# Two groups of attention values as one product in seven parts, in a hybrid decoder layer

## Chip, cores and metric

The kernel runs on one core of one Trainium2 chip. The metric is the device time of one execution in microseconds (us), given as the median of several runs.

## The reference

The reference is one decoder layer over 512 tokens of width 1024: a SwiGLU block, a mixer of two branches, and a second SwiGLU block, each with a normalisation before and after. The part that matters here is the attention branch. The normalised input `u` (512 x 1024) is multiplied by `w_in`, and columns 3072 to 4607 of it are the values of three groups of heads, 512 columns for each group:

```python
u = rms_norm(h, mix_norm_pre[l])
proj = u @ w_in[l]
q, k, v, xr, yr, gl = jnp.split(proj, splits, axis=-1)
...
v = v.reshape(B, S, N_GROUPS, HEADS_PER_GROUP, HEAD_DIM)
```

Queries and keys are made in the same way from other columns. Each group then attends with its own dilation, and the three results are merged. All is float32.

## The kernel before

A float32 product is made of three matmuls: each operand is split into a high part (ScalarE copies it into a rounded format) and a low part (VectorE subtracts, `split`, lines 295 to 297), and high x high, high x low and low x high are accumulated in PSUM. A weight of 1024 columns per partition thus costs one ScalarE copy and one VectorE subtraction of 128x1024 before TensorE can use it.

Many products are made with seven block products where eight would be the plain way (a Strassen-like scheme). For this both operands are cut into halves in two directions, and sums of the quarters, called *forms*, are split. `forms_of` (line 576) makes the seven forms of the input, p1 to p7, in three steps: `early` makes three sums (lines 615 to 617), `middle` splits p6 and p5 with one sum between them (620 to 622), `late` splits p7 and p4 (625 and 626). p1, p2 and p3 are parts of the input as it is. `w_forms` (632) makes the forms of a pair of weight tiles, and `seven` (697) runs the products of a pair of query and key tiles.

The weights come as one stream of 1 MB blocks in the order in which they are needed (`stream_plan`, line 101). `raw_of` (234) issues the next block on SyncE's queue into one of two `raw` buffers; `fetch` (254) splits a block's part into one of four `w8` buffers (2 x 1024 columns each).

The order of the instructions on each engine is laid out ahead of time by a list scheduler: it goes by the place in the program, and a block under `tc.high_priority(offset=...)` moves forward by that many instructions. `AHEAD` is 100 and stands around the preparation of weights; `EVAC` is 200 and stands around copies out of PSUM. On the chip each engine then keeps to its order.

The mixer begins while the first block's normalisation ends: `Boundary.block` normalises 128 tokens, `Boundary.turn` (506) transposes them on TensorE and splits them into the input `um`. Then `values(g)` (1072) makes the values of a group: four blocks of 128 tokens, each with its own PSUM bank, over eight chunks of 128 input rows, three matmuls each (lines 1086 to 1088) with 128 tokens of the input as the stationary operand and 512 columns of weights as the moving one. Group 0 goes block by block, because the last blocks of the input are still being normalised; its values are afterwards moved by 16 small DMAs into another order (1108). Groups 1 and 2 go chunk by chunk over all four blocks, and ScalarE copies the four banks out (1102). The steps of the input's forms stand between the groups in the program (lines 1115, 1117, 1122): `early` after group 0, `middle` after group 1, `late` after group 2 and after the preparation of the first pair. Queries and keys (`qk`, 1131) follow, one pair per group and head, each with the next pair's preparation ahead of it (`pair_of`, 1124).

[...] `facc` is a buffer of 128 x 8 x 512 that holds the transposed input while the forms are made.

Of the kernel before, what the change touches and what calls it, by code (L numbers as in the profile page):

```python
# [10 lines left out]
F32 = mybir.dt.float32  # L11
# [5 lines left out]
P = 128  # L17
# [19 lines left out]

LAST = 384
WARM = 10
VALUES = (0, 1, 2)  # L40
QKB = 6
CB = 6
GATE1 = ((), (0, 1), (2, 3, 4), (5, 6, 7))
# [57 lines left out]
def stream_plan():  # L101

    plan = []

    def down(n, a, half):
        for kk in range(part_blocks(a)):
            plan.append((("down", n, a, half, kk), 1024))

    def ffn(n):
        for ev in ffn_order(n):  # L110
            if ev[0] == "std":
                plan.append((("gate", n, ev[1]), 1024))
                plan.append((("up", n, ev[1]), 1024))
            elif ev[0] == "prep":
                plan.append((("gu", n, ev[1]), 2048))
            elif ev[0] == "down":
                down(n, *ev[1:])
            elif ev[0] == "prepd":
                for q in SEVEN_RAW[ev[2]]:
                    plan.append((("dq", n, ev[1], q), 1024))  # L120
        for half in range(2):
            down(n, len(FF_PARTS) - 1, half)

    def values(g):
        for k in range(4):
            plan.append((("v", g, k), 1024))

    def qk(h):
        for g in range(NG):
            plan.append((("pair", g * 4 + h, 12 + g * 4 + h), 2048))  # L130

    ffn(1)
    del plan[:4]
    for k in range(KC):
        plan.insert(k, (("start", k), 512))
    for g in VALUES:
        values(g)
    for h in range(NH):
        qk(h)
    for c in range(0, KC, 2):  # L140
        plan.append((("pair", 52 + c, 53 + c), 2048))
    for m in range(0, KC, 2):
        plan.append((("attn", m), 1024))
    for what, h in LRU_ORDER:
        if what == "gates":
            plan.append((("lru", h), 1024))
        elif (what, h) in PAIRED:
            plan.append((pair_key(what, h), 2048))
        else:
            for c in GATE1[h] if what == "gate1" else (2 * h, 2 * h + 1):  # L150
                plan.append((("in", COLUMN[what] + c), 1024))
    for m in range(KC):
        plan.append((("rec", m), 1024))
    for half in range(2):
        for kk in range(4):
            plan.append((("out", half, kk), 1024))
    ffn(2)
    return plan
# [25 lines left out]
def hybrid_layer(ctx: ExitStack, tc: tile.TileContext, xT: bass.AP, xN: bass.AP, wst: bass.AP,  # L184
# [46 lines left out]
    groups = stream_groups()  # L231
    state = {"g": 0, "i": 0, "off": 0, "raw": None, "ahead": AHEAD}

    def raw_of(key):

        g, i = state["g"], state["i"]
        grp = groups[g]
        if i == 0:
            w = grp[-1][1] + grp[-1][2]
            raw = wpool.tile([P, RAW_W], F32, name="raw", tag="raw", bufs=2)  # L240
            src = bass.AP(tensor=wst.tensor, offset=wst.offset + state["off"], ap=[[w, P], [1, w]])
            nc.sync.dma_start(raw[:, :w], src)
            state["raw"] = raw
            state["off"] += w * P
        k, o, w = grp[i]
        assert k == key, (k, key)
        src = state["raw"][:, o:o + w]
        if i + 1 == len(grp):
            state["g"], state["i"] = g + 1, 0
        else:  # L250
            state["i"] = i + 1
        return src

    def fetch(key, slot=None, ahead=0):

        with tc.high_priority(offset=ahead if slot else state["ahead"]):
            src = raw_of(key)
            w = src.shape[-1]
            t = slot() if slot else w8() if w > 512 else w4()
            split(t[:, 0, :w], t[:, 1, :w], src)  # L260
            return t[:, 0, :w], t[:, 1, :w]
# [795 lines left out]
    with ExitStack() as mx:  # L1057
# [11 lines left out]

        vals = {}  # L1070

        def values(g, first=False):
            if g:
                vals[g] = apool.tile([P, 4, T], F32, name="vals", tag=f"v{g}")
            else:
                vals[g] = tpl.tile([P, 8, T], F32, name="vals", tag="attn")[:, 0:4, :]
            ws = [fetch(("v", g, k)) for k in range(4)] if first else [None] * 4
            pss = [acc_ps() for _ in range(4)] if g != VALUES[1] else [aux_ps(), aux_ps(), aux_ps(), acc_ps()]

            def part(kk, bs):  # L1080
                wh, wl = (w.rearrange("p (k c) -> p k c", k=2) for w in ws[kk])
                for b in bs:
                    bl = slice(b * P, (b + 1) * P)
                    for i in range(2):
                        k = 2 * kk + i
                        PE.matmul(pss[b], um.hi[k][:, bl], wh[:, i, :], start=k == 0, stop=False)  # L1086
                        PE.matmul(pss[b], um.hi[k][:, bl], wl[:, i, :], start=False, stop=False)  # L1087
                        PE.matmul(pss[b], um.lo[k][:, bl], wh[:, i, :], start=False, stop=k == KC - 1)  # L1088

            if first:  # L1090
                for b in range(4):
                    for kk in range(4):
                        part(kk, (b,))
                    if b < 2:
                        bd1.turn(b + 2)
                    ACT.activation(vals[g][:, b, :], pss[b], AF.Copy)
            else:
                for kk in range(4):
                    ws[kk] = fetch(("v", g, kk))
                    part(kk, range(4))  # L1100
                for b in range(4):
                    ACT.activation(vals[g][:, b, :], pss[b], AF.Copy)
            if g == 0:

                nv = apool.tile([P, 4, T], F32, name="vals", tag="vn")
                for b in range(4):
                    for p in range(4):
                        nc.gpsimd.dma_start(nv[32 * p:32 * p + 32, b, :], vals[g][32 * b:32 * b + 32, p, :])
                vals[g] = nv

        t, steps = forms_of(um, um_t[:2], um_t[2:], apool, False, rec_half)
        values(VALUES[0], True)
        attn_t = tpl.tile([P, 8, T], F32R, name="attn", tag="attn")
        attn = Act([attn_t[:, i, :] for i in range(4)], [attn_t[:, 4 + i, :] for i in range(4)])
        steps[0]()
        values(VALUES[1])
        steps[1]()
        values(VALUES[2])
        pairs = [[(g * 4 + hd, 12 + g * 4 + hd) for g in range(NG)] for hd in range(NH)]
        order = [("pair",) + p for ps in pairs for p in ps] + [("pair", 52 + c, 53 + c) for c in range(0, KC, 2)]  # L1120
        forms = {order[0]: w_forms(order[0])}
        steps[2]()

        def pair_of(key):

# [433 lines left out]
def _block(key, a):  # L1559
    kind = key[0]  # L1560
    if kind in ("gate", "up"):
        return _cols(a[f"ffn{key[1]}_w_{kind}"], key[2] * P)
    if kind in ("down", "out"):
        if kind == "out":
            w, r0, half = a["w_out"], key[2] * 2 * P, key[1]
        else:
            w, r0, half = a[f"ffn{key[1]}_w_down"], (FF_PARTS[key[2]][0] + key[4] * 2) * P, key[3]
        return w[r0:r0 + 2 * P, half * T:(half + 1) * T].reshape(2, P, T).transpose(1, 0, 2)
    if kind == "dq":
        half, i = "gu".index(key[3][0]), int(key[3][1])  # L1570
        r0 = (FF_PARTS[key[2]][0] + 2 * i) * P
        return a[f"ffn{key[1]}_w_down"][r0:r0 + 2 * P, half * T:(half + 1) * T].reshape(2, P, T).transpose(1, 0, 2)
    if kind == "gu":
        u, g = (_cols(a[f"ffn{key[1]}_w_{k}"], key[2] * P) for k in ("up", "gate"))
        return np.concatenate([u, g], axis=1)
    if kind == "in":
        return _cols(a["w_in"], key[1] * P)
    if kind == "v":
        return _cols(a["w_in"][key[2] * 256:(key[2] + 1) * 256], 3072 + key[1] * 512, 512)
    if kind == "pair":  # L1580
        u, g = (_cols(a["w_in"], c * P) for c in (key[2], key[1]))
        return np.concatenate([u, g], axis=1)
    if kind == "start":
        k = key[1]
        rows = slice(k * P, (k + 1) * P)
        return np.stack([a["ffn1_w_" + n][rows, f * P:(f + 1) * P] for f in (0, 1) for n in ("gate", "up")], 1)
    if kind == "lru":
        w = np.stack([a["lru_w_x"][key[1]], a["lru_w_a"][key[1]]])
        return w.reshape(2, 2, P, 256).transpose(2, 0, 1, 3)
    if kind == "attn":  # L1590
        return np.concatenate([_cols(a["w_attn_branch"], (key[1] + i) * P) for i in range(2)], axis=1)
    return _cols(a["w_rec_branch"], key[1] * P)
# [39 lines left out]
```

## Time and profile before

| | us |
|---|---|
| median of 3 runs | 1225.06 |
| lowest and highest run | 1224.48, 1225.47 |
| the profiled execution | 1223.49 |
| its span, first to last instruction | 1221.7 |

| engine | busy, us | share of the span |
|---|---|---|
| PE (TensorE, matmuls) | 1212.1 | 99% |
| PEld (TensorE, weight loads) | 1106.7 | 91% |
| DVE (VectorE) | 988.4 | 81% |
| ACT (ScalarE) | 790.4 | 65% |

The durations come from the profiled execution, which is one run; the median is taken over others. A row of a timeline gives the start and the duration in us, the engine, the line of the kernel, what is written and read, how many such instructions follow one another, and in brackets how long the engine stood idle before and what ended it. The values of groups 1 and 2 begin at 371.76 us.

### The profile page before, as it was taken

To read this page: it belongs to the slowest core of one execution; us is meant where nothing else is said; L and a number is where in the kernel's file an instruction comes from. 1 tells how busy PE (TensorE), PEld (TensorE's weight loads), DVE (VectorE), ACT (ScalarE), POOL (GpSimd) and SP (SyncE) were. 2 spreads that over 40 slices of the span, in tenths; PEclk is the share of its full clock that TensorE was granted. 3 is DMA by queue.
4 is the path that set the end of the run, shared out by engine and by line. 5 is a ranking of instruction groups with operands and counts; after the bars stand their busy time and mean duration, and the time that the engine had idled before them with its cause. 6 is when DMAs were issued, how large, how long until landed. Compare 5 with 4: busy or idle time off the path is not lost.

```text
span 1221.7 us, 19429 instructions
## 1 busy us (share of the span) xinstructions
PE 1212.1 (99%) x7790; PEld 1106.7 (91%) x7790; DVE 988.4 (81%) x1518; ACT 790.4 (65%) x1353; POOL 26.1 (2%) x51
## 2 busy tenths in 40 slices
PE   9999999999999999999999999999999999999997
PEld 8899999999888899999989888878899999999996
DVE  7988888899685587888765897785798888889975
ACT  7556777777564465665735887834566677878752
POOL 0000000000011000000000000000100000000000
PEclk9999999999999999999999999999999999999999
DMA  6223333334623222222225222234443333333341
GB/s 247 95 81 119 121 121 122 121 122 169 243 92 126 99 83 104 79 81 101 80 95 192 83 104 83 90 115 167 152 154 122 121 122 122 121 122 122 138 173 69
DMA packets 29403, 148.75 MB, mean 122 GB/s; under 512 B 3200, under 2 KB 6400, under 8 KB 15232
## 3 DMA queue, kind: packets, MB, share of 16 engines
q1 hardware_dynamic: 22032, 130.20, 29.8%
q0 software_dynamic: 7280, 17.30, 4.2%
q8 instruction: 61, 1.00, 0.3%
q14 instruction: 30, 0.25, 0.1%
HBM read 137.01 MB, written 6.29 MB: 117 GB/s over the span
## 4 chain that ended last, share of the span: by engine, by line
PE 92%; DVE 4%; ACT 3%; issue 0%; DMA 0%; DVEq 0%
PE acc L664 15%; PE acc L665 15%; PE acc L666 14%; PE acc L310 6%; PE acc L309 6%; PE acc L311 6%; PE aux L933 4%; PE aux L934 3%; PE aux L935 3%; PE acc L424 3%; PE acc L425 3%; PE acc L423 3%; PE acc L1087 1%; PE acc L1088 1%; PE acc L1086 1%; DVE w L297 1%
## 5 line engine op out<-in xcount | busy, mean ns | idle before, releaser
L297 DVE TENSOR_TENSOR w<-raw,w 128x1024 fp32r<-128x1024 f32 (+1 forms) x272 | 297.7, 1099 | 83.1 <-ACT w L296 78.1
L664 PE MATMUL acc<-big,w 128*128 128x256 f32 x1248 | 354.2, 284 | 0.2 <-ACT c L678 0.2
L665 PE MATMUL acc<-big,w 128*128 128x256 f32 x1248 | 354.1, 284 | 0.0
L666 PE MATMUL acc<-big,w 128*128 128x256 f32 x1248 | 353.7, 283 | 0.0
L296 ACT ACTIVATE w<-raw 128x1024 fp32r<-128x1024 f32 (+1 forms) x272 | 259.4, 957 | 111.6 <-PE acc L311 33.9
L664 PEld LDWEIGHTS acc<-big,w 128*128 128x128 f32 x1248 | 239.2, 192 | 2.5 <-ACT c L678 0.9
L665 PEld LDWEIGHTS acc<-big,w 128*128 128x128 f32 x1248 | 239.3, 192 | 1.5
L666 PEld LDWEIGHTS acc<-big,w 128*128 128x128 f32 x1248 | 239.3, 192 | 0.0
L933 PE MATMUL aux<-w,xf 128*128 128x512 f32 x196 | 76.4, 393 | 0.8 <-ACT w L296 0.8
L934 PE MATMUL aux<-w,xf 128*128 128x512 f32 x196 | 76.6, 391 | 0.0
L935 PE MATMUL aux<-w,xf 128*128 128x512 f32 x196 | 76.3, 389 | 0.0
L296 ACT ACTIVATE w<-s 128x1024 fp32r<-128x1024 f32 (+1 forms) x57 | 58.4, 1028 | 20.9 <-PE acc L666 13.4
L297 DVE TENSOR_TENSOR w<-s,w 128x1024 fp32r<-128x1024 f32 (+1 forms) x57 | 67.3, 1183 | 5.0 <-ACT w L296 4.8
L641 DVE TENSOR_TENSOR s<-raw 128x512 f32<-128x512 f32 x55 | 37.8, 687 | 32.4 <-DMA raw<-in_w 32.4
L309 PE MATMUL acc<-big,w 128*128 128x512 f32 x160 | 62.3, 389 | 0.0
L310 PE MATMUL acc<-big,w 128*128 128x512 f32 x160 | 62.3, 389 | 0.0
L311 PE MATMUL acc<-big,w 128*128 128x512 f32 x160 | 62.2, 389 | 0.0
L678 ACT ACTIVATE c<-acc 128x256 f32<-128x256 f32 x74 | 28.2, 382 | 37.3 <-PE acc L666 37.0
L841 ACT ACTIVATE g<-g 128x256 f32<-128x256 f32 x35 | 14.6, 416 | 50.1 <-DVE g L840 50.1
L708 ACT ACTIVATE c<-acc 128x256 f32<-128x256 f32 x72 | 27.3, 380 | 30.1 <-PE acc L666 28.9
L311 PE MATMUL acc<-xf,w 128*128 128x512 f32 (+1 forms) x136 | 46.1, 339 | 0.0
L310 PE MATMUL acc<-xf,w 128*128 128x512 f32 (+1 forms) x136 | 46.0, 339 | 0.0
(396 smaller groups left out, 2772.0 us busy)
## 6 DMA issues: line engine op xcount, KB each, us to landing
raw<-in_w SPq DMA_DIRECT2D x110, 1024.0 KB, 4.8
raw<-in_w SPq DMA_DIRECT2D x14, 512.0 KB, 3.5
big<-xf POOLq DMA_DIRECT2D x6, 512.0 KB, 3.5
gains<-in_rows POOLq DMA_DIRECT2D x5, 512.0 KB, 5.4
h<-in_x SPq DMA_DIRECT2D x8, 256.0 KB, 5.1
h<-in_xn POOLq DMA_DIRECT2D x4, 512.0 KB, 5.6
kept_m<-h POOLq DMA_DIRECT2D x4, 512.0 KB, 2.9
h<-kept_m POOLq DMA_DIRECT2D x4, 512.0 KB, 4.6
```

What stands on the lines that cost most here:

```text
L296: ACT.activation(dh, src, AF.Copy)
L297: DVE.tensor_sub(dl, src, dh.bitcast(F32))
L309: PE.matmul(ps, wh, xh, start=first, stop=False)
L310: PE.matmul(ps, wh, xl, start=False, stop=False)
L311: PE.matmul(ps, wl, xh, start=False, stop=last)
L641: DVE.tensor_add(s12[1], u0, u1)
L664: PE.matmul(ps, wh, xh, start=start and k == 0, stop=False, skip_group_check=True)
L665: PE.matmul(ps, wh, xl, start=False, stop=False, skip_group_check=True)
L666: PE.matmul(ps, wl, xh, start=False, stop=k == 3, skip_group_check=True)
L933: PE.matmul(ps, xh, wh, start=first and j == 0, stop=False, skip_group_check=True)
L934: PE.matmul(ps, xh, wl, start=False, stop=False, skip_group_check=True)
L935: PE.matmul(ps, xl, wh, start=False, stop=j == 1, skip_group_check=True)
```

## The change

Group 0 stays as it is (`values_first`, with the same instructions). Groups 1 and 2 are made together in `values_two`. Their weights are cut into four quarters of 512 rows x 512 columns: g0 and g1 are the upper and lower rows of group 1, u0 and u1 those of group 2. Tokens are cut into two halves. The result is thus a product of halves by halves, and it is made with the seven products p1 to p7 on the forms of the input that queries and keys use. Each product has two blocks of 128 tokens, four chunks of 128 rows and three matmuls of 512 columns.

The forms of the weights are made from the four quarters: w1 = g0, w2 = g1, w5 = u0 + u1, w6 = that + g0, w7 = u0 + g0, w3 = w6's sum + g1, w4 = u1. Each form takes two `w8` buffers, and so two ScalarE copies and two VectorE subtractions of 128x1024. Each of the four sums is two VectorE additions of 128x1024. g0 and g1 are loaded into the two `raw` buffers, u0 and u1 into the tiles that later hold the values of groups 1 and 2; the running sum lies in the unused half of the tile for group 0's values. Between the products, sums pass from bank to bank by ScalarE's copies, and two partial results are kept in `facc`. The steps of the input's forms stand at other places: `early` ahead of p1, `middle` behind p1, `late` behind p5. The first pair's preparation stands behind p3.

The core of the diff, without the rewriting of group 0's loop:

```diff
-    for g in VALUES:
-        values(g)
+    for k in range(4):
+        plan.append((("v", 0, k), 1024))
+    for q in ("g0", "g1", "u0", "u1"):
+        plan.append((("vq", q), 2048))
...
-    def raw_of(key):
+    def raw_of(key, dst=None):
...
-            raw = wpool.tile([P, RAW_W], F32, name="raw", tag="raw", bufs=2)
+            raw = dst if dst is not None else wpool.tile([P, RAW_W], F32, name="raw", tag="raw", bufs=2)
...
+        def values_two(steps, then):
+            def v_of(g):
+                return apool.tile([P, 4, T], F32, name="vals", tag=f"v{g}")
...
+            def add(dst, x, y):
+                with tc.high_priority(offset=AHEAD):
+                    for h in range(2):
+                        cs = slice(h * D, h * D + D)
+                        DVE.tensor_add(dst[:, cs], x[:, cs], y[:, cs])
+            def form(src):
+                with tc.high_priority(offset=AHEAD):
+                    ws = [w8(), w8()]
+                    for h, w in enumerate(ws):
+                        split(w[:, 0, :], w[:, 1, :], src[:, h * D:h * D + D])
+                return ws
+            def prod(p, w, pss, start):
+                for j, ps in enumerate(pss):
+                    for k in range(4):
+                        xh, xl = (x[:, k, j * P:j * P + P] if len(x.shape) == 3 else x[:, k, j, :] for x in t[p])
+                        wh, wl = (w[k // 2][:, i, k % 2 * T:k % 2 * T + T] for i in range(2))
+                        PE.matmul(ps, xh, wh, start=start and k == 0, stop=False, skip_group_check=True)
+                        PE.matmul(ps, xh, wl, start=False, stop=False, skip_group_check=True)
+                        PE.matmul(ps, xl, wh, start=False, stop=k == 3, skip_group_check=True)
+            def copies(dsts, pss, scale=1.0):
+                with tc.high_priority(offset=EVAC):
+                    for dst, ps in zip(dsts, pss):
+                        ACT.activation(dst, ps, AF.Copy, scale=scale)
+            with tc.high_priority(offset=AHEAD):
+                g0, g1 = raw_of(("vq", "g0")), raw_of(("vq", "g1"))
+                u0 = raw_of(("vq", "u0"), flat(v_of(1)))
+                u1 = raw_of(("vq", "u1"), flat(v_of(2)))
+            sd = flat(both[:, 4:8, :])
+            b, y, z = [aux_ps(), aux_ps()], [acc_ps(), acc_ps()], [aux_ps(), acc_ps()]
+            c5, c6 = ([facc[:, i + j, :] for j in range(2)] for i in (0, 2))
+            w1, w2 = form(g0), form(g1)
+            steps[0]()
+            add(sd, u0, u1)
+            prod("p1", w1, b, True)
+            copies(y, b)
+            w5 = form(sd)
+            steps[1]()
+            add(sd, sd, g0)
+            prod("p2", w2, y, False)
+            w6 = form(sd)
+            add(u0, u0, g0)
+            prod("p5", w5, z, True)
+            copies(c5, z)
+            w7 = form(u0)
+            add(sd, sd, g1)
+            steps[2]()
+            prod("p6", w6, b, False)
+            copies(c6, b)
+            w3 = form(sd)
+            vals[1] = v_of(1)
+            copies([vals[1][:, j, :] for j in range(2)], y)
+            prod("p7", w7, b, False)
+            v = [acc_ps(), acc_ps()]
+            copies(v, b)
+            w4_ = form(u1)
+            vals[2] = v_of(2)
+            for j in range(2):
+                DVE.scalar_tensor_tensor(vals[2][:, 2 + j, :], b[j], -1.0, c5[j], op0=ALU.mult, op1=ALU.subtract)
+            prod("p3", w3, z, False)
+            then()
+            for j in range(2):
+                DVE.tensor_add(vals[1][:, 2 + j, :], z[j], c6[j])
+            prod("p4", w4_, v, False)
+            copies([vals[2][:, j, :] for j in range(2)], v, -1.0)
...
-        steps[0]()
-        values(VALUES[1])
-        steps[1]()
-        values(VALUES[2])
...
-        forms = {order[0]: w_forms(order[0])}
-        steps[2]()
+        forms = {}
+        def first_forms():
+            forms[order[0]] = w_forms(order[0])
+        values_two(steps, first_forms)
...
+    if kind == "vq":
+        g, half = "gu".index(key[1][0]), int(key[1][1])
+        return _cols(a["w_in"][half * T:half * T + T], 3072 + (g + 1) * 512, 512)
```

More of the change, by code (lines that the diff above doesn't have):

```diff
@@ L39 @@
 WARM = 10
-VALUES = (0, 1, 2)
 QKB = 6
@@ L122, in ffn @@
             down(n, len(FF_PARTS) - 1, half)
-    def values(g):
-        for k in range(4):
-            plan.append((("v", g, k), 1024))
     def qk(h):
@@ L1070, in hybrid_layer @@
         vals = {}
[L1072 to L1109, printed above, removed]
@@ L1111, in hybrid_layer, with values_first @@
-        t, steps = forms_of(um, um_t[:2], um_t[2:], apool, False, rec_half)
-        values(VALUES[0], True)
+        both = tpl.tile([P, 8, T], F32, name="vals", tag="attn")
+        def values_first():
+            v = both[:, 0:4, :]
+            ws = [fetch(("v", 0, k)) for k in range(4)]
+            pss = [acc_ps() for _ in range(4)]
+            for b in range(4):
+                bl = slice(b * P, (b + 1) * P)
+                for k in range(KC):
+                    wh, wl = (w.rearrange("p (k c) -> p k c", k=2)[:, k % 2, :] for w in ws[k // 2])
+                    PE.matmul(pss[b], um.hi[k][:, bl], wh, start=k == 0, stop=False)
+                    PE.matmul(pss[b], um.hi[k][:, bl], wl, start=False, stop=False)
+                    PE.matmul(pss[b], um.lo[k][:, bl], wh, start=False, stop=k == KC - 1)
+                if b < 2:
+                    bd1.turn(b + 2)
+                ACT.activation(v[:, b, :], pss[b], AF.Copy)
+            nv = apool.tile([P, 4, T], F32, name="vals", tag="vn")
+            for b in range(4):
+                for p in range(4):
+                    nc.gpsimd.dma_start(nv[32 * p:32 * p + 32, b, :], v[32 * b:32 * b + 32, p, :])
+            vals[0] = nv
@@ new lines, in values_two, with flat @@
+        def values_two(steps, then):
+            def v_of(g):
+                return apool.tile([P, 4, T], F32, name="vals", tag=f"v{g}")
+            def flat(v):
+                return v.rearrange("p k t -> p (k t)")
+            def add(dst, x, y):
[62 more added lines that the diff above has]
+            copies([vals[2][:, j, :] for j in range(2)], v, -1.0)
@@ L1113, in hybrid_layer @@
+        t, steps = forms_of(um, um_t[:2], um_t[2:], apool, False, rec_half)
+        values_first()
+        pairs = [[(g * 4 + hd, 12 + g * 4 + hd) for g in range(NG)] for hd in range(NH)]
+        order = [("pair",) + p for ps in pairs for p in ps] + [("pair", 52 + c, 53 + c) for c in range(0, KC, 2)]
+        forms = {}
+        def first_forms():
+            forms[order[0]] = w_forms(order[0])
+        values_two(steps, first_forms)
         attn_t = tpl.tile([P, 8, T], F32R, name="attn", tag="attn")
@@ L1114, in hybrid_layer @@
         attn = Act([attn_t[:, i, :] for i in range(4)], [attn_t[:, 4 + i, :] for i in range(4)])
-        steps[0]()
-        values(VALUES[1])
-        steps[1]()
-        values(VALUES[2])
-        pairs = [[(g * 4 + hd, 12 + g * 4 + hd) for g in range(NG)] for hd in range(NH)]
-        order = [("pair",) + p for ps in pairs for p in ps] + [("pair", 52 + c, 53 + c) for c in range(0, KC, 2)]
-        forms = {order[0]: w_forms(order[0])}
-        steps[2]()
         def pair_of(key):
```

## The prediction

> **What bounds the kernel now.** I read the page first: the engines' shares, the clock row, the chain that ended last.
>
> ```profile
> span 1221.7 us, 19429 instructions
> PE 1212.1 (99%) x7790; PEld 1106.7 (91%) x7790; DVE 988.4 (81%) x1518; ACT 790.4 (65%) x1353; POOL 26.1 (2%) x51
> ...
> PEclk9999999999999999999999999999999999999999
> ...
> PE 92%; DVE 4%; ACT 3%; issue 0%; DMA 0%; DVEq 0%
> ```
>
> TensorE is the bound: 92% of the chain, at full clock throughout. A matmul saved there is time saved, as long as VectorE (81% over the whole span) still delivers the operands in time. So the stage itself has to be looked at. I took the busy times of three stretches (columns: us, PE, PEld, DVE, ACT, POOL, clock, DMA share, GB/s): from the last transposed block of the input to the end of group 0's values; groups 1 and 2; the first pairs of queries and keys.
>
> ```profile
> 364.00:371.80 7.80, 7.80 (x36) 6.44 (x36) 7.69 (x7) 6.79 (x8) 4.66 (x10) 1.00 0.37 93
> 371.76:415.30 43.54, 43.54 (x194) 36.06 (x193) 19.71 (x21) 14.83 (x19) 1.98 (x4) 1.00 0.33 116
> 416.50:446.00 29.50, 29.50 (x248) 29.47 (x247) 24.27 (x36) 15.96 (x26) 0.00 (x0) 1.00 0.23 77
> ```
>
> In the middle row, the stage that is changed, PE has no gap and DVE works 19.71 of 43.54 us. In the last row DVE already works 24.27 of 29.50 (82%), so what is left over from the stage can be caught up there only slowly.
>
> Next the pitch of its matmuls: the first of groups 1 and 2 from PE's timeline, and the row of line 1088, whose last one starts at 415.0.
>
> ```profile
> 371.76 0.39 PE L1086 MATMUL aux<-w,big 128*128 128x512 f32 x1
> ```
>
> ```profile
> L1088 PE MATMUL acc<-w,big x72: 387/389/482, 348.1 to 415.0; 128*128 128x512 f32 x72
> ```
>
> The duration of 0.39 us overlaps with its neighbours. From the first start to the last lie 191 steps, (415.0 - 371.76)/191 = 0.226 us each. That pitch is the price of one matmul, not 0.389.
>
> **What goes from PE.** Before: 2 groups x 4 blocks x 8 chunks x 3 matmuls = 192. After: 7 products x 2 blocks x 4 chunks x 3 = 168, of the same 128x512 form. 24 fewer x 0.226 = **5.4 us**; each product lasts 24 x 0.226 = 5.4 us too. A product accumulates into a bank that ACT seeded, and reads the input's forms as blocks of 128 contiguous columns as before; I cost both at nothing, because the pitch in the row above is that of accumulating matmuls with such blocks. If the whole saving comes, the stage ends at 409.9 and not at 415.3.
>
> [...]
>
> **What DVE gets.** DVE's timeline of the stretch, and ACT's, give the prices; the waits of 344 to 420 us follow.
>
> ```profile
> 362.51 1.29 DVE L514 TENSOR_TENSOR big<-aux,big 128x512 fp32r<-128x512 f32 x2 [1.15 <-ACT big L513]
> 363.98 1.23 DVE L615 TENSOR_TENSOR ts<-facc 128x1024 f32<-128x1024 f32 x1 [0.18 <-ACT facc L515]
> ...
> 369.87 4.63 DVE L297 TENSOR_TENSOR w<-raw,w 128x1024 fp32r<-128x1024 f32 x4
> 374.41 1.22 DVE L621 SCALAR_TENSOR_TENSOR ts<-ts,facc 128x1024 f32<-128x1024 f32 x1
> ...
> 378.54 1.23 DVE L297 TENSOR_TENSOR w<-raw,w 128x1024 fp32r<-128x1024 f32 x1 [0.55 <-ACT w L296]
> 383.99 1.23 DVE L297 TENSOR_TENSOR w<-raw,w 128x1024 fp32r<-128x1024 f32 x1 [4.22 <-ACT w L296]
> ...
> 401.39 0.68 DVE L641 TENSOR_TENSOR s<-raw 128x512 f32<-128x512 f32 x1
> 401.99 0.68 DVE L646 TENSOR_TENSOR raw<-s,raw 128x512 f32<-128x512 f32 x1
> ...
> 405.75 1.23 DVE L297 TENSOR_TENSOR w<-s,w 128x1024 fp32r<-128x1024 f32 x1 [1.26 <-ACT w L296]
> 411.19 1.23 DVE L297 TENSOR_TENSOR w<-raw,w 128x1024 fp32r<-128x1024 f32 x1 [4.21 <-ACT w L296]
> ```
>
> ```profile
> 369.86 3.16 ACT L296 ACTIVATE w<-raw 128x1024 fp32r<-128x1024 f32 x3
> 372.92 0.58 ACT L1096 ACTIVATE vals<-acc 128x512 f32<-128x512 f32 x1
> ```
>
> ```profile
> DVE w L297 <- ACT w L296: 25.1, 8, 4.2
> ACT w L296 <- PE acc L1088: 20.6, 8, 4.4
> ```
>
> - Four splits in a row take 4.63 with the last at 1.22, so one 128x1024 operation on DVE costs 1.14 us in a row; from L641 to L646 a 128x512 one costs 0.60.
> - Six more splits of the weights (14 for 8) and eight adds of 128x1024 (four calls, two halves each): 14 x 1.14 = 16.0 us. Four more DVE operations take results out of PSUM, 128x512, as L514's two take 1.29: 4 x 0.65 = 2.6 us.
> - ACT gets six copies at 1.05 (3.16/3) and, with 12 copies out of PSUM where there were 8, four more at 0.6: 8.7 us on 6.79 + 14.83 = 21.6. That is 30.3 of 45.9 us, 66%; it hides.
>
> DVE's sum from 364.0, when the input is complete: 7.69 + 19.71 = 27.4 now; plus 16.0 and 2.6 makes **46.0 us, where 409.9 - 364.0 = 45.9 us are left.** So DVE goes from half idle to full. Two things in the 27.4 need not be done by 409.9: the adds for the second pair (three at 0.6) and the last split of the first pair (1.1), which is needed in that pair's fifth product. That leaves 43.1 of 45.9.
>
> [...]
>
> **Does each product find its operands?** With no stall the products p1, p2, p5, p6, p7, p3, p4 start at 371.8, 377.2, 382.6, 388.1, 393.5, 398.9 and 404.4. I count in 128x1024 operations of 1.14 us on DVE from 364.0.
> - p1 and p2 want two splits each, like the weights of group 1 before: the row at 369.87 shows them done by 374.5. Nothing changes there.
> - Up to p5: three sums of the input's forms, w1, w2, the first add, w5 and p5's form of the input: 12 operations, 13.7 of 18.6 us.
> - Up to p6: five more, 19.4 of 24.1. Up to p7: six more (an add, w7, L621, p7's form), 26.2 of 29.5, a margin of 3.3 us.
> - Up to p3: 30.8 of 34.9, and p4: 34.2 of 40.4.
>
> So the sums fit, and p7 is tightest, because its form of the input comes from the third step, which has no raised priority. What may stand ahead of it in DVE's queue and isn't needed for it: the last add (2.3), the first pair's adds (1.8), p4's form (1.1). All together 5.2 makes p7 late by 5.2 - 3.3 = 1.9 us; none of it, 0. I take the middle, **1.0 us**.
>
> The buffers that hold split weights are four, two for a product. So a form can be made during the product before its own: slots come free 1.4 us before and at the end of the product that last used them, and one product (5.4 us) then covers a form of two copies and two splits, 1.05 + 1.14 + 1.14 = 3.3 us, with 2.1 to spare. A form begun only when its product is due would cost those 3.3.
>
> **Loads.** The two u halves go into the tiles of the values, behind the two g halves on SP's queue. No row shows when those tiles' memory is free. The latest release I can see is line 502's last read of the gains, 361.4.
>
> ```profile
> raw<-in_w SPq DMA_DIRECT2D x8, 1024.0 KB, 4.8
> ```
>
> ```profile
> 359.95 1.42 DVE L502 SCALAR_TENSOR_TENSOR u<-h,stat,gains 128x512 f32<-128x512 f32 x2
> ```
>
> Two such loads, one after the other, end at 361.4 + 9.6 = 371.0. The add that needs them has to be over with w5 by 382.6: it starts at about 374.5, behind w2, so the load costs nothing even at the late end. At the early end (landed before 360) the add could slip into the normalisation's chain ahead of 362 and push L514 back by one or two times 1.14. Group 0's fourth block needs L514's result at 366.3 (24 matmuls of 0.226 back from 371.76), and it is there at 363.8: 2.5 us of cover for 2.3. So both ends give nothing, the early one barely.
>
> **Into queries and keys.** The first pair's splits wait for slots of p3 and p4, its third until 408.5 (six matmuls before the end); before, the third ended at 412.4 (the row at 411.19) with the stage at 415.3. It is needed at 409.9 + 4 x 1.4 (a pair's seven products take about 9.6 us) so it is in time. Up to 2.9 us (46.0 - 43.1) of adds and splits come later than now into a stretch with 18% free: between 0 and 2.9, I take **0.3**, near the low end, because only what comes behind a product's deadline can cost; a gain is excluded, since nothing there is done earlier than now.
>
> **Sum:** -5.4 + 1.0 + 0.3 = **-4.1 us**. The profiled execution took 1223.49 us (span 1221.7 and 1.8 around it), so 1219.4 for it; it lies 1.6 below the median of 1225.06, so the median becomes **1221.0**. Bounds of the forecast: all saved, 1219.6; 1.9 + 2.9 lost, 1224.5.
>
> **Rivals.** A measurement of this kernel can tell about 0.2%, 2.45 us, from no change: faster is below 1222.6, slower above 1227.5.
>
> 1. *DVE is the stage's bound.* All 46.0 us must be done in the stage, and at each of the five later forms DVE stands 0.55 us as at 378.54: 48.8 against 45.9, 2.9 us late, plus the 1.0 at p7. -5.4 + 3.9 = -1.5: **1223.6**. For it: the full sum. Against it: the 2.9 us that can come later, and 3 to 6 us of margin at most products.
> 2. *Waits in order on DVE: slower.* The waits above show DVE standing at splits for ACT's copy, and ACT for PE to free a slot; now this costs nothing, since nothing useful is behind. After, what stands behind such a split are adds and input forms that would be ready. If before each of the seven forms DVE stands for one copy, 1.26 us as in the row at 405.75, the stage needs 46.0 + 8.8 = 54.8 against 45.9: 8.9 us of stall, +3.5: **1228.6**. It turns into a loss when the standing exceeds 5.3 us in all, 0.76 per form. For it: a fixed order, and 25.1 us of such standing in the stretch now. Against it: adds and forms of the input are ready in most of those moments, and where two splits follow each other only the first stands. [...]
> 3. *The products don't save what they say.* If the 168 matmuls had a pitch of 43.5/168 = 0.259, nothing would be won: **1225**. PEld's row (36.06 of 43.54 us) leaves room, so I hold this unlikely.
>
> **How the numbers follow.** Forecast 0.60 (mostly below 1222.6; a tail of 0.04 above it, with 2 and more us lost at p7 and after it), rival 1 0.18 (0.05 of it below 1222.6), rival 2 0.19, rival 3 0.03. Faster 0.56 + 0.05 = 0.61; same 0.04 + 0.13 + 0.03 = 0.20; slower 0.19. The range starts at 1219.3, 0.3 below full saving for the spread of the runs, takes in rivals 1 and 3 and the part of rival 2 up to 1227.5.
>
> **What would show it.** Right: a stretch of 168 matmuls of about 38 us plus 1 of gaps; DVE above 90% busy in it; the largest PE gap in front of p7, ended by a DVE form of the input or ACT's copies behind it. Wrong: PE gaps in front of p5, p6, p3 or p4, ended by a split of weights that stood for a slot (rival 2); gaps in the first pairs of more than 1 us (the leftover undervalued); group 0's fourth block late behind an add; a pitch other than 0.226.

## The result and the profile after

The changed kernel takes **1219.30 us** (median of 6 runs, 1218.55 to 1220.15) against 1224.72 of the kernel before (6 runs, 1224.39 to 1225.47): ratio 0.9955, interval 0.9942 to 0.9968. That is 5.4 us, where 4.1 were forecast: about the whole price of the 24 matmuls, and at the lower edge of the range.

The page after, with the engines' shares, the clock and the chain that ended last:

```profile
span 1217.7 us, 19414 instructions
PE 1207.9 (99%) x7766; PEld 1102.5 (91%) x7766; DVE 1005.8 (83%) x1536; ACT 797.5 (65%) x1363; POOL 26.1 (2%) x51
...
PEclk9999999999999999999999999999999999999999
...
PE 83%; DVE 8%; ACT 6%; issue 1%; DMA 1%; DVEq 0%; ACTq 0%
```

24 matmuls fewer, 17 us more of DVE, and TensorE is still busy throughout. The chain's share of DVE has doubled, but not in the part that was changed: from 364.9 to 411.0 us the chain holds matmuls alone. In another profile of the same kernel (`after_again`, below) the chain has 89% of PE and 5% of DVE, so these shares of the whole span say nothing of the change. The stage itself has to be read.

The three stretches that were read before (columns: us, PE, PEld, DVE, ACT, POOL, clock, DMA share, GB/s). This execution reaches the first product 0.92 us later than the one before did (372.68, not 371.76), in a part that the change doesn't touch, so stretches are compared by their lengths:

```profile
364.90:372.70 7.80, 7.80 (x36) 6.43 (x36) 7.69 (x7) 6.78 (x8) 4.20 (x10) 1.00 1.00 325
372.67:410.80 38.13, 38.13 (x169) 31.30 (x168) 36.38 (x38) 22.45 (x29) 2.49 (x6) 1.00 0.21 69
412.00:441.50 29.50, 29.50 (x248) 29.50 (x248) 24.36 (x37) 16.01 (x25) 0.00 (x0) 1.00 0.35 112
```

In the stage DVE went from 19.71 of 43.54 us to 36.38 of 38.13, 95%. The stretch of the first pairs looks as it did. On PE's timeline the last matmul of group 0, the first product, p7's beginning and the first pair are these:

```profile
372.45 0.39 PE L1082 MATMUL acc<-w,big 128*128 128x512 f32 x1
372.68 0.39 PE L1120 MATMUL aux<-w,big 128*128 128x512 f32 x1
...
375.17 0.80 PE L1121 MATMUL aux<-w,big 128*128 128x512 f32 x2
375.80 0.40 PE L1122 MATMUL aux<-w,big 128*128 128x512 f32 x1
...
394.45 0.39 PE L1122 MATMUL aux<-w,rb 128*128 128x512 f32 x1
394.68 0.39 PE L1120 MATMUL aux<-w,big 128*128 128x512 f32 x1
...
411.00 0.28 PE L661 MATMUL acc<-big,w 128*128 128x256 f32 x1
```

The stage lasts 411.00 - 372.68 = **38.32 us**, where it lasted 415.28 - 371.76 = 43.52: 5.20 less. The first pair's start in the kernel before is this row of its PE timeline:

```profile
415.28 0.28 PE L664 MATMUL acc<-big,w 128*128 128x256 f32 x1
```

Only one place breaks the pitch of 0.227, in p1: from 375.17 to 375.80 two matmuls take 0.63, 0.18 too much. In front of p7 (394.45 to 394.68) there is no gap. DVE's order explains both (timeline of DVE):

```profile
370.78 1.22 DVE L294 TENSOR_TENSOR w<-raw,w 128x1024 fp32r<-128x1024 f32 x1
371.91 1.22 DVE L1106 TENSOR_TENSOR vals<-vals 128x1024 f32<-128x1024 f32 x1
373.05 3.49 DVE L294 TENSOR_TENSOR w<-raw,w 128x1024 fp32r<-128x1024 f32 x3
...
386.95 2.36 DVE L1106 TENSOR_TENSOR vals<-vals,raw 128x1024 f32<-128x1024 f32 x2
...
392.63 0.68 DVE L638 TENSOR_TENSOR s<-raw 128x512 f32<-128x512 f32 x1
393.23 1.22 DVE L294 TENSOR_TENSOR big<-facc,big 128x1024 fp32r<-128x1024 f32 x1
...
396.75 1.22 DVE L294 TENSOR_TENSOR rb<-ts,rb 128x1024 fp32r<-128x1024 f32 x1
```

One half of the first sum (371.91) got in between the splits of w1, which is p1's gap. Before p7's form (393.23) stand the last sum (386.95) and one small sum of the first pair (392.63), but not p4's form (396.75). It ends at 394.45, **0.23 us before p7**. The last row of waits below is that gap of p1. And the waits show what became of DVE's standing at splits, first in the stage before (371.7 to 415.3 us), then after (372.6 to 411 us):

```profile
DVE w L297 <- ACT w L296: 20.9, 7, 4.2
```

```profile
DVE w L294 <- ACT w L293: 1.8, 3, 1.3
...
PEld aux L1121 <- DVE w L294: 0.3, 1, 0.3
```

### The profile page after: what moved, and what is told of

Read it like the earlier page. It is cut to its first block, busy times and chain, and to the rows that moved or that the text cites. A ratio compares the mean times of both kernels' runs of the same rounds, so it can differ in the third digit from the quotient of the medians.

```text
span 1217.7 us, 19414 instructions
## 1 busy us (share of the span) xinstructions
PE 1207.9 (99%) x7766; PEld 1102.5 (91%) x7766; DVE 1005.8 (83%) x1536; ACT 797.5 (65%) x1363; POOL 26.1 (2%) x51
## 4 chain that ended last, share of the span: by engine, by line
PE 83%; DVE 8%; ACT 6%; issue 1%; DMA 1%; DVEq 0%; ACTq 0%
PE acc L661 15%; PE acc L662 14%; PE acc L663 14%; PE acc L307 4%; PE acc L306 4%; PE acc L308 4%; PE aux L930 3%; PE aux L931 3%; PE aux L932 3%; PE acc L422 3%; PE acc L421 3%; PE acc L420 3%; DVE w L294 2%; DVE sig L1424 1%; ACT w L293 1%
## 5 line engine op out<-in xcount | busy, mean ns | idle before, releaser
L294 DVE TENSOR_TENSOR w<-raw,w 128x1024 fp32r<-128x1024 f32 (+1 forms) x268 | 293.0, 1098 | 60.1 <-ACT w L293 55.1
L293 ACT ACTIVATE w<-raw 128x1024 fp32r<-128x1024 f32 (+1 forms) x268 | 255.1, 956 | 95.7 <-PE acc L308 33.7
```

What stands on the lines that cost most here:

```text
L293: ACT.activation(dh, src, AF.Copy)
L294: DVE.tensor_sub(dl, src, dh.bitcast(F32))
```

## The experiments

After the result two theories stood against each other. **A**, the prediction's frame: TensorE's pitch sets the stage, and DVE costs only where a form is late for its product (deadlines). **B and C**: DVE, busy 95%, sets the stage, by its total (C) or altogether (B). The row of each run is its stage, from the first product's start to the first pair's, from the stretches; the changed kernel's is this:

```profile
372.68:411.00 38.32, 38.32 (x170) 31.46 (x169) 36.44 (x39) 22.54 (x29) 2.48 (x6) 1.00 0.21 68
```

**An eighth product** (`e1_eighth`).

```diff
+            prod("p4", w4_, [aux_ps(), aux_ps()], True)
             prod("p4", w4_, v, False)
```

> The changed kernel with an eighth product: p4's 24 matmuls are issued a second time into two banks that nothing reads. Theory A (TensorE alone sets the stage, one matmul costs its pitch of 0.226 us): 5.4 us more than the changed kernel, which is the time of the kernel before within 0.5 us. Theory B (VectorE holds the stage, so a product more gives it time to catch up): clearly less than 5.4, some 3 to 4 us.

```profile
373.56:417.29 43.73, 43.73 (x193) 35.97 (x192) 36.45 (x39) 22.59 (x29) 2.09 (x5) 1.00 0.18 58
```

1224.55 us, ratio to the kernel before 1.0002 (0.9993 to 1.0010); stage 43.73, 5.41 more. 24 matmuls cost 5.41 us in the trace, 0.225 each, with DVE's 36.45 us unchanged beside them. So the stage's gain of 5.20 is the price of these matmuls, less 0.2; B would have made them cheaper.

**Without the weights' sums** (`e2_no_sums`).

```diff
-            add(sd, u0, u1)
...
-            w5 = form(sd)
+            w5 = form(u0)
...
-            add(sd, sd, g0)
...
-            w6 = form(sd)
-            add(u0, u0, g0)
+            w6 = form(g0)
...
-            add(sd, sd, g1)
...
-            w3 = form(sd)
+            w3 = form(g1)
```

> The changed kernel without the four sums of weight quarters (eight additions of 128x1024, 9.1 us of VectorE); the forms w5, w6, w7 and w3 are split from u0, g0, u0 and g1 instead, so the values of groups 1 and 2 are not the reference's. Theory A: at most 0.3 us faster than the changed kernel, namely the gap of 0.23 us that the first sum causes in p1. Theory B (VectorE holds the stage at 95% busy): 1 us or more faster.

```profile
372.13:410.21 38.08, 38.08 (x170) 31.54 (x168) 28.01 (x31) 22.65 (x29) 2.37 (x5) 1.00 0.22 68
```

1219.00 us (0.9954, 0.9942 to 0.9967); the stage loses 0.24 us: the gap in p1 (0.18) and the slightly wider steps behind it. DVE's 36.44 us became 28.01, and TensorE gained nothing else. 38.08/168 = 0.2267 is the bare pitch. The eight additions are hidden but for 0.24 us; B falls.

**More VectorE work ahead of p7's form** (`e3_more1`, `e3_more2`, `e3_more6`, n = 1, 2, 6).

```diff
+            def same(v, n):
+                with tc.high_priority(offset=AHEAD):
+                    for i in range(n):
+                        cs = slice(i % 2 * D, i % 2 * D + D)
+                        DVE.tensor_tensor(v[:, cs], v[:, cs], v[:, cs], op=ALU.max)
...
             add(sd, sd, g1)
+            same(sd, n)
             steps[2]()
```

> The changed kernel with one VectorE operation of 128x1024 more (the maximum of the running sum with itself, which leaves it as it is) behind the last sum, ahead of p7's form of the input in VectorE's order. Theory A with deadlines: p7's form ends 0.23 us before p7 begins, so 1.14 more make p7 late by 0.9, and the kernel by 0.9 us. Rival C (only the total counts: 36.4 us busy of 38.1, 1.7 free): no change.

> The changed kernel with two more VectorE operations of 128x1024 (2.3 us) behind the last sum, ahead of p7's form of the input; in VectorE's order one split of w3 comes ahead of it too. Theory A with deadlines: p7's form is late by 2.3 + 1.1 - 0.2 = 3.2 us; TensorE's order brings eight of p3's matmuls (1.8 us) forward, so 1.4 us more than the changed kernel. Rival C (only VectorE's total counts): 36.4 + 2.3 - 38.1 = 0.6 us more at most, and nothing if the pairs' sums come later.

> The same with six such operations, 6.8 us. In VectorE's order p7's form now also stands behind w3's two splits. Theory A with deadlines: p7 late by 6.8 + 2.3 - 0.2 = 8.9 us, the kernel by 7 to 9 us. Rival C (total): 36.4 + 6.8 - 38.1 = 5.1 us more, or less, since work for the pairs can come later.

```profile
373.06:411.76 38.70, 38.60 (x169) 31.39 (x168) 37.73 (x40) 22.65 (x29) 2.62 (x6) 1.00 0.21 67
```

```profile
372.80:412.00 39.20, 38.58 (x169) 31.38 (x168) 38.86 (x41) 22.65 (x29) 2.21 (x5) 1.00 0.20 65
```

```profile
372.84:417.89 45.05, 40.63 (x170) 32.48 (x168) 42.87 (x44) 22.80 (x29) 2.21 (x5) 0.96 0.18 57
```

| extra DVE work, us | median, us | ratio to before (interval) | stage against 38.32, us | expected by A, by C |
|---|---|---|---|---|
| 1.1 | 1220.05 | 0.9961 (0.9948 to 0.9973) | +0.38 | +0.9, 0 |
| 2.3 | 1220.29 | 0.9969 (0.9957 to 0.9980) | +0.88 | +1.4, up to +0.6 |
| 6.8 | 1226.87 | 1.0015 (1.0006 to 1.0024) | +6.73 | +7 to 9, +5.1 |

Each lies above C and below A. With one operation, half of the 0.38 is a longer gap in p1 (0.37 for 0.18), which lies 14 us ahead of the extra work and is not its price (see the run without the raised priority, below), and p7 itself costs only some 0.1 to 0.2, though its form is late. PE's timeline there, and the form on DVE's:

```profile
395.26 0.39 PE L1126 MATMUL aux<-w,big 128*128 128x512 f32 x1
395.49 0.39 PE L1127 MATMUL aux<-w,big 128*128 128x512 f32 x1
395.71 0.39 PE L1126 MATMUL aux<-w,big 128*128 128x512 f32 x1
395.94 0.46 PE L1126 MATMUL acc<-w,big 128*128 128x512 f32 x1
396.24 0.49 PE L1128 MATMUL aux<-w,big 128*128 128x512 f32 x1
```

```profile
394.95 1.23 DVE L294 TENSOR_TENSOR big<-facc,big 128x1024 fp32r<-128x1024 f32 x1
```

The form ends at 396.18, 0.92 after p7's start at 395.26. But what DVE makes of a form is its low part, and only the third matmul (line 1128) needs it; in front of it the order has two matmuls of p3, which are independent. Four matmuls of 0.227 fill the 0.92. So A needs an amendment: *a late form costs its lateness less the matmuls that stand before its low part is used.* This run alone shows it by itself. In the run with 2.3 us the rule gives 0.9 (the form ends at 397.94, 3.18 after p7's start at 394.76, with ten matmuls in between), and 0.88 was measured; but there a copy out of PSUM is what ends the wait that shows (0.62 us before the matmul at 396.21), at 395.56 on ACT. It overwrites a part of `facc` that line 618's sum reads (393.85 to 395.07, behind the extra work), and it stands behind two other copies on ACT (from 394.61); which of the two held it up isn't separated. In the run with 6.8 us the two waits that show on TensorE (3.17 and 1.25 us, rows in the last section) end with ScalarE's copy of w3's high part and with that same copy into `facc`. w3 is split from the running sum that the extra work rewrites, and a matmul of p3 that stood between p7's had to wait for it. So there it is w3's deadline that shows, and not p7's form alone.

**The same work with p7's form ahead of it** (`e4_p7_first_more2`, `e4_p7_first_more6`, n = 2, 6).

```diff
-            steps[1]()
+            with tc.high_priority(offset=AHEAD):
+                steps[1]()
...
+            with tc.high_priority(offset=AHEAD):
+                steps[2]()
             w7 = form(u0)
             add(sd, sd, g1)
-            steps[2]()
+            same(sd, n)
```

> The same two extra operations in the same place, but the second and third step of the input's forms have the raised priority and the third stands ahead of the last sum, so that p7's form and the sum before it are ready before the extra work. Theory A with deadlines: nothing is due behind the extra work but w7's second half, whose lateness of about 1.2 us is filled by six matmuls brought forward: 0 to 0.3 us more than the changed kernel, 1 us and more below the run in which the same work stands ahead of p7's form. Rival C: the same time as that run.

> As before with six extra operations (6.8 us). Theory A with deadlines: w7's second half about 1 us late after the matmuls brought forward, then w3's two splits 2.4 us late behind the extra work: 3 to 4 us more than the changed kernel, where the same work ahead of p7's form took 7.6 more. Rival C: the total stays the same, so 7 to 8 us more again.

```profile
372.56:411.13 38.57, 38.57 (x169) 31.38 (x168) 38.35 (x40) 22.71 (x29) 2.34 (x5) 1.00 0.21 67
```

```profile
372.99:414.40 41.41, 39.17 (x169) 31.23 (x168) 41.09 (x41) 22.61 (x29) 2.42 (x5) 1.00 0.20 63
```

| extra DVE work, us | form behind it: stage | form ahead of it: stage | median, us (ratio, interval) |
|---|---|---|---|
| 2.3 | 39.20 | 38.57 | 1219.72 (0.9962, 0.9950 to 0.9975) |
| 6.8 | 45.05 | 41.41 | 1224.01 (0.9995, 0.9986 to 1.0003) |

The same work costs 0.25 us in one place of the order and 0.88 in the other; with 6.8 us, 3.09 and 6.73. 0.25 and 3.09 are as A expected; but at 2.3 us the two places are 0.63 apart, where 1 us and more was expected. With 6.8 us TensorE's waits (0.43, 0.76 and 1.05 us) end with the splitting of w7 and w3, the forms that stand behind the extra work. C, by which the place does not matter, falls: at 6.8 us the intervals of the two ratios lie apart, while at 2.3 us they overlap and the trace alone shows it. DVE also kept to the order laid out for it where the form stands behind the extra work: as expected from that order, one split of w3 (394.98) precedes p7's form (396.72) with 2.3 us, and two (from 399.56) precede it (402.43) with 6.8.

**Without the raised priority** (`e6_noprio`): the three `tc.high_priority(offset=AHEAD)` in `values_two` become `offset=0`.

> The changed kernel without the raised priority of the weights' loads, sums and forms of the two groups. TensorE's order stays the same; on VectorE the sum ahead of p7's form and that form move forward. Theory A with deadlines: every form is still there in time, so no change (within 0.3 us). Rival 2 of the prediction (the order alone keeps VectorE from standing at splits): 2 us or more slower.

```profile
372.73:411.39 38.66, 38.37 (x169) 31.45 (x168) 36.68 (x39) 22.77 (x29) 2.50 (x6) 1.00 0.22 68
```

1219.99 us (0.9959, 0.9946 to 0.9973), stage 0.34 longer, of which p1's gap, now 0.45, makes the most. This is near the 0.3 that A allowed and far from rival 2's two and more. The raised priority hardly matters to this stage. The longer gap goes with a later load, not with the priority: the second u half landed at 371.91 (9.1 us after its issue), DVE stood 0.31 us, and the first sum began at 372.35, 0.44 after the landing, with w1's next split behind it. In the run with one extra operation the landing was at 372.05 and the sum began at 372.49, again 0.44 later, and p1's gap was longer too. In the changed kernel the landing was at 371.45 and the sum began at 371.91, with no idle time of DVE.

**The order tidied** (`e5_tidy`), with the changed kernel once more beside it (`after_again`).

```diff
-            add(sd, u0, u1)
+            for h in range(2):
+                cs = slice(h * D, h * D + D)
+                DVE.tensor_add(sd[:, cs], u0[:, cs], u1[:, cs])
...
-            steps[1]()
+            with tc.high_priority(offset=AHEAD):
+                steps[1]()
...
+            with tc.high_priority(offset=AHEAD):
+                steps[2]()
             w7 = form(u0)
             add(sd, sd, g1)
-            steps[2]()
```

> The changed kernel with the first sum of the weights at normal priority (it then stands behind w1's and w2's splits) and the second and third step of the input's forms at the raised one (p7's form then stands ahead of the last two sums). Theory A with deadlines: the gap of 0.2 us in p1 goes and nothing else changes, so the stage of the two groups takes 168 x 0.227 = 38.1 us and the kernel 0 to 0.3 us less than the changed one, within the spread of the runs. Rival C: nothing changes at all.

> The changed kernel once more, on the same chip as the run above, as its measure. Theory A: 5.2 us below the kernel before, of which 24 x 0.227 = 5.4 are saved matmuls and 0.2 a gap in p1. Theory of chance (the 5.4 us of the first measurement are 4 of the change and the rest the spread of its runs): about 4 us below it.

```profile
372.48:410.79 38.31, 38.31 (x170) 31.46 (x168) 36.64 (x39) 22.73 (x29) 2.44 (x5) 1.00 0.22 69
```

```profile
372.87:411.24 38.37, 38.37 (x169) 31.45 (x168) 36.51 (x39) 22.54 (x29) 2.63 (x6) 1.00 0.21 68
```

1219.37 us tidied (0.9951, 0.9937 to 0.9965) and 1220.13 for the changed kernel (0.9959, 0.9945 to 0.9973), with 1225.56 for the kernel before. The intervals overlap, and the stages are 38.31 and 38.37, so the tidied one can't be called better. Its gap in p1 is gone, but w5, which now waits for the first sum, is a little late in p5 (rows of PE there: 386.30 to 386.60 and 386.60 to 386.94 instead of 0.23 each). The wait was moved, not removed; my 38.1 was wrong. The changed kernel's gain is 5.43 us here and its stage 5.15 us shorter than 43.52, as theory A says. The time alone doesn't exclude the theory of chance: the interval is 3.3 to 6.7 us and holds its 4 as well. The stage does, at 5.20 and 5.15 us in two traces.

## Why the prediction was off

- **The saved matmuls: right.** 5.4 forecast; the eighth product measures 5.41, and without the sums the stage is 43.52 - 38.08 = 5.44 shorter. The pitch, not the duration, was the price.
- **DVE's sum: right.** 46.0 us were forecast from the end of the input to the first pair, 43.1 of them pressing, in 45.9. The two stretches after hold 7.69 + 36.38 = 44.1, between the two.
- **p7 is the tightest product: right. Its price of 1.0 us: the step that failed.** I bounded the lateness by 0 (nothing ahead of p7's form) and 1.9 (all 5.2 us ahead, less the margin of 3.3) and took the middle of the two prices. But the price is zero up to 3.3 us and rises only then: the middle of the *work*, 2.6 us, costs nothing. The order put 2.9 us ahead (the last sum 2.3 and one small sum 0.6), the form ended 0.23 before p7, and p7 paid 0.00. The largest gap of TensorE, which I had looked for in front of p7, was in p1. Where extra work made the form late by 0.92, p7 paid 0.1 to 0.2, since the low part is needed by the third matmul first and TensorE's order put independent ones in between. I had taken the products to run strictly one after the other. One reading was also wrong without changing the price: the sum of line 621 makes p4's form, not p7's, so both the margin and the work that may stand ahead are one operation (1.1 us) larger than I wrote.
- **0.3 us in the first pairs: also nothing.** From the first pair to the first matmul of the scores it takes 30.23 us in both (415.28 to 445.51 and 411.00 to 441.23), and 30.23 or 30.24 in every run above, even with 6.8 us more on DVE. The adds that come later find their place.
- **p1: "Nothing changes there" was wrong by 0.2 us.** The first sum stood between w1's splits in VectorE's order. It did so without the raised priority too (gap 0.45); where it stands behind the splits, in `e5_tidy`, p1 has no gap.
- **The load: issued at the late end, as forecast, but not always free.** The u halves were issued when the last read of the gains was over (it ended at 362.27, and the issue began at 362.34; SP's timeline, below). I had the first sum behind w2; it stood behind w1's first half, at 371.91, 0.46 after the second landing and with no idle time in front of it, so here the load cost nothing. There is no margin left at that place: where it landed later, p1's gap was 0.37 and 0.45.

```profile
362.34 0.80 SPq L239 DMA_DIRECT2D vals<-in_w  x2
363.19 0.43 SPq L1215 DMA_DIRECT2D bs<-in_bias  x1
```

- **The rivals.** Rival 1 (DVE the bound) would have paid 3.9 us; it pays 0.24. Rival 2 (standing in order) needed 8.8 us of standing; the three waits that are left make 1.8, because adds and forms were ready to be put there. Without the sums (`e2_no_sums`) DVE stood 9.7 us at splits in the stage. Rival 3 (another pitch) is excluded by 38.08/168 = 0.2267.
- **The range.** Its lower end was full saving less 0.3 for the runs' spread, with every unknown of DVE counted as a loss above it. The measured time fell on that edge: 5.44 saved, 0.24 paid, and the rest the runs' spread, with the kernel before itself at 1224.35 to 1225.56 in the four sets of runs made since. The stage's 5.2 us is what the trace shows; the other 0.2 of the 5.4 stays within that spread.

## What to carry to other kernels

A cost that only appears beyond a margin is not half of its worst case: put the likely amount of work against the margin first, and price what is over. An engine busy 95% of a stage need not bound it; look for each result's deadline, and for the first of the consumer's instructions that needs its last part. And take the gain of fewer matmuls by their pitch, with the other engines' total as a second check, not as the first.

## What was not expected of the hardware

A gap on TensorE was followed by a slower clock. In the run with six operations ahead of p7's form TensorE stood 3.17 and 1.25 us, and after that seven starts in a row came at nearly twice the pitch. Some rows of its PE timeline, and the stretch after the gaps:

```profile
398.58 0.50 PE L1126 MATMUL aux<-w,big 128*128 128x512 f32 x1 [3.17 <-ACT w L293]
400.33 0.57 PE L1126 MATMUL acc<-w,big 128*128 128x512 f32 x1 [1.25 <-ACT facc L1133]
...
402.69 0.63 PE L1126 MATMUL aux<-w,big 128*128 128x512 f32 x1
403.12 0.63 PE L1127 MATMUL aux<-w,big 128*128 128x512 f32 x1
```

```profile
401.00:404.50 3.50, 3.50 (x10) 2.73 (x11) 3.50 (x5) 0.71 (x1) 0.00 (x0) 0.57 0.00 0
```

The granted clock was 0.57 from 401.0 to 404.5, and matmuls came every 0.43 us: 7 x (0.43 - 0.23) = 1.4 us of that run's 6.7. With the form ahead of the extra work the gaps were 1.2 us at most, and the clock was 1.00 in the stretches behind them. So 1.4 of the 3.6 us between those two runs is the clock that followed the gap, and not the deadline itself; that the gap lowered the clock is the order of events in one trace, and no run was made for it alone. In all 11 executions of that kernel the mean granted clock is 0.995 to 0.997, where it is 0.998 or 0.999 with one or two extra operations in that place, which suggests that each of the 11 has such a stretch.
